# The second layer's conditioning product moved from VectorE, ScalarE and GpSimd to column groups of TensorE

## The chip, the core and the metric

The kernel runs on one core of one Trainium2 chip. The metric is the device time of one execution, in microseconds (us). Three executions of the kernel before took 2191.03, 2194.42 and 2195.73 us; the median is 2194.42 us.

A core has engines with a queue of instructions each: TensorE (PE in the profile, with PEld for its weight loads), VectorE (DVE), ScalarE (ACT), GpSimd (POOL) and SyncE (SP, which here only issues transfers). An engine takes its instructions in the order in which the program holds them; an instruction that waits for a semaphore holds everything behind it on its engine. GpSimd both computes and issues transfers, in one queue.

## The reference, cut to what matters

Two layers (`DEPTH = 2`) of a backbone over 512 latent and 256 context tokens, 1024 wide, in fp32. Each layer has six modulation vectors of 1024 values for each of two conditioning vectors:

```
mod_x = silu(c) @ ada_w[l] + ada_b[l]          # ada_w[l]: 1024 x 6144
mod_c = silu(c_ctx) @ ada_w[l] + ada_b[l]
sh1, sc1, g1, sh2, sc2, g2 = split_cols(mod, (D_MODEL,) * 6)
u   = modulate(rmsnorm(x, norm1_w[l]), sh1, sc1)
x   = x + g1 * mix(u)
x   = x + g2 * sq_relu_mlp(modulate(rmsnorm(x, norm2_w[l]), sh2, sc2), w_mlp1[l], w_mlp2[l])
```

The conditioning product is small in arithmetic (two rows times a 1024 x 6144 matrix) and reads 25 MB of `ada_w` for each layer.

## The kernel before, in words

Activations stand in SBUF as tiles of 128 rows. The big matrix products run on TensorE as three passes of a high and a low half (`mm3`, lines 302 to 305: high by high, low by high, high by low). Every weight slab is loaded by SP as a raw tile `wr`, copied to its high half `wh` by ScalarE (L139), and its low half `wl` is made by VectorE or GpSimd (L140). These pieces are handed out one by one (`W.tick()`) between the products.

The place that matters is the MLP of layer 0, which is a generator `mlp_gen`: for eight chunks of 512 hidden units a first product (`mlp1`, into PSUM tiles `ph`), and for six of them a second product in Strassen's form (`strassen`, seven products into PSUM tiles `st`, whose operands `ob` are made by VectorE and ScalarE from the hidden tile `hb`, L1192 to L1197, and whose results are added up by VectorE, L1226). GpSimd combines the Strassen weights (L152). After the sixth of these a `fold` adds the result to the residual, and the last two chunks follow.

While this MLP runs, the conditioning product of layer 1 is made beside it (lines 1331 to 1334). There are 12 pieces of 512 columns (`ada`, six vectors in two halves), each from two transfers of 1 MB (`ada_load`, L338, issued by GpSimd into a tile `adaw` of the pool `big`, which has 11 buffers that the MLP's tiles share). Each time that a piece yields, the `Filler` puts out a number of microseconds of MLP work:

```
for _ in chainup(*[ada(l + 1, v, c0, 512, ps, "t", wk, None, E1) for v in range(6) for c0 in (0, 512)]):
    fm.adv(8.0)
```

`E1` is ScalarE, so the pieces of layer 1 go through `ada_dve` (L310): the row of `silu(c)` is multiplied in by VectorE (L327, L329), eight instructions for each piece; the row of `silu(c_ctx)` by ScalarE (L323) and added up by GpSimd (L325). Both leave a 128 x 512 partial sum, `acc`, whose 128 rows TensorE then adds with a selector of ones (L356), in four column groups of 32 columns: `tile_position=(0, 32 * g)`. Then VectorE copies the result (`adar`, L371 or L376), and it is transposed (L380) into `cols` or written to DRAM (`grow`, L374).

In layer 0 most pieces take another way through the same function: L362 multiplies the loaded tile on TensorE, with `cT` (the two conditioning rows and 30 columns of zeros) as the stationary side, again in four column groups.

The order of the instructions on each engine is not written by hand. The framework's scheduler places them when the program is built, from the order in which the generators put them out and its own estimate of when each is ready.

Of the kernel before, what the change touches and what calls it, by code (L numbers as in the profile page):

```python
# [9 lines left out]
F32 = mybir.dt.float32  # L10
F32R = mybir.dt.float32r
I32 = mybir.dt.int32
AF = mybir.ActivationFunctionType
ALU = mybir.AluOpType
# [3 lines left out]
P = 128  # L18
DM = 1024
# [29 lines left out]
def kernel(  # L49
# [26 lines left out]
    nc = tc.nc  # L76
    V, A, T = nc.vector, nc.scalar, nc.tensor
# [5 lines left out]
    def bigt(name, dt=F32):  # L83
        return big.tile([P, 4, TOK], dt, name=name, tag="big")

    def flat(t):
        return t.rearrange("p a b -> p (a b)")

    class Weights:
# [73 lines left out]
        def next(self, key):  # L163
            i = self.i
            want, (src, *_) = self.plan[i][:2]
            assert want == key, (want, key)
            while self.bg and self.bg[0][0] <= i:
                self.tick()
            self.dma(i + 3)
            self.split(i + 2)  # L170
            self.i += 1
            k, n = src.shape[1], src.shape[2]
            return tuple(t[:, : k * n].rearrange("p (k n) -> p k n", k=k) for t in self.sp.pop(i))
# [131 lines left out]
        T.matmul(ps, al, bh, start=False, stop=last, **kw)  # L305

    lda = [None]
    E0, E1 = {(3, 0): V, (4, 0): V, (5, 0): V}, A

    def ada_dve(l, v, c0, wk, eng1):  # L310
        at = wk.tile([P, DM], F32, name=f"acc{l}{v}{c0}", tag="xn" if l else "jk", bufs=2 if l else 1)
        acc = [at[:, 0:512], at[:, 512:DM]]
        if eng1 is A:
            tm = wk.tile([P, DM], F32, name=f"acm{l}{v}{c0}", tag="xn", bufs=2)
        for s, (rv, ins) in enumerate(ada_load(l, v, c0, 512, nc.gpsimd)):
            lda[0] = getattr(ins, "ins", ins)
            for k in range(4):
                kk = 4 * s + k
                for st, eng in ((0, V), (1, eng1)):
                    w = cT[:, kk, st : st + 1]  # L320
                    if eng is A:
                        h = tm[:, 512 * (kk % 2) : 512 * (kk % 2) + 512] if kk else acc[st]
                        A.activation(out=h, in_=rv[:, k, :], func=AF.Copy, scale=w)  # L323
                        if kk:
                            nc.gpsimd.tensor_tensor(out=acc[st], in0=acc[st], in1=h, op=ALU.add)  # L325
                    elif kk == 0:
                        eng.tensor_scalar(out=acc[st], in0=rv[:, k, :], scalar1=w, scalar2=None, op0=ALU.mult)  # L327
                    else:
                        eng.scalar_tensor_tensor(out=acc[st], in0=rv[:, k, :], scalar=w, in1=acc[st], op0=ALU.mult, op1=ALU.add)  # L329
            yield None  # L330
        return acc

    def ada_load(l, v, c0, n, eng):
        kp = 2048 // n
        for s in range(KT // kp):
            rw = big.tile([P, 6, 512], F32, name=f"adaw{l}{v}{c0}{s}", tag="big")
            rv = rw.rearrange("p a b -> p (a b)")[:, : kp * n].rearrange("p (k n) -> p k n", k=kp)
            yield rv, eng.dma_start(out=rv, in_=wslab(ada_w[l], s * kp * P, kp, v * DM + c0, n))  # L338

    def ada(l, v, c0, n, ps_pool, ps_tag, wk, loads=None, eng1=None):  # L340
        G = n // P
        kp = 2048 // n
        gate = v in (2, 5)
        acc = None
        if eng1 is not None:
            g = ada_dve(l, v, c0, wk, eng1)
            while acc is None:
                try:
                    next(g)
                    yield 1.0  # L350
                except StopIteration as e:
                    acc = e.value
        pa = ps_pool.tile([P, 512], F32, name=f"ada{l}{v}{c0}", tag=ps_tag)
        for st in range(2 if acc else 0):
            for g in range(G):
                T.matmul(pa[32 * g : 32 * g + 32, :P], sel[:, 1 - st : 33 - st], acc[st][:, P * g : P * g + P],  # L356
                         start=(st == 0), stop=(st == 1 and not gate), skip_group_check=True, tile_position=(0, 32 * g))
        for s, (rv, ins) in enumerate(() if acc else loads or ada_load(l, v, c0, n, nc.gpsimd)):
            lda[0] = getattr(ins, "ins", ins)
            for k in range(kp):  # L360
                for g in range(G):
                    T.matmul(pa[32 * g : 32 * g + 32, :P], cT[:, kp * s + k, :], rv[:, k, P * g : P * g + P],  # L362
                             start=(s + k == 0), stop=(kp * s + k == KT - 1 and not gate), skip_group_check=True, tile_position=(0, 32 * g))
            yield 1.0
        row = wk.tile([P, P], F32, name=f"adar{l}{v}{c0}", tag="rt", bufs=2)
        if gate:
            for g in range(G):
                o = 16 + 8 * v + c0 // P + g
                T.matmul(pa[32 * g : 32 * g + 32, :P], wcol[l][:, o : o + 1].to_broadcast([P, 32]), ident, start=False, stop=True,
                         skip_group_check=True, tile_position=(0, 32 * g))  # L370
            V.tensor_copy(row, pa[:, :P])  # L371
            for g in range(G):
                o = c0 + P * g
                nc.gpsimd.dma_start(out=grow[l][v // 3, :, o : o + P], in_=row[32 * g : 32 * g + 2, :])  # L374
        else:
            V.tensor_copy(row[: 32 * G], pa[: 32 * G, :P])  # L376
            vi = {0: 0, 1: 1, 3: 2, 4: 3}[v]
            ks = slice(c0 // P, c0 // P + G)
            pt = ps_pool.tile([P, 512], F32, name=f"adat{l}{v}{c0}", tag=ps_tag)
            T.transpose(pt[:, : 32 * G], row[: 32 * G], ident[: 32 * G, : 32 * G])  # L380
            dst = cols[l][:, vi, ks, :]
            src = pt[:, : 32 * G].rearrange("p (g q) -> p g q", g=G)[:, :, 0:2]
            bias = wcol[l][:, 16 + 8 * v : 24 + 8 * v][:, ks]
            V.tensor_tensor(out=dst, in0=src, in1=bias.unsqueeze(2).to_broadcast([P, G, 2]), op=ALU.add)
            if v in (1, 4):
                nw = (wcol[l][:, 0:8] if v == 1 else wcol[l][:, 8:16])[:, ks]
                V.scalar_tensor_tensor(out=dst, in0=dst, scalar=1.0, in1=nw.unsqueeze(2).to_broadcast([P, G, 2]), op0=ALU.add, op1=ALU.mult)
        yield 0.5

    def load_rows(l, wk, eng):  # L390
        rows = wk.tile([68, P], F32, name=f"lrows{l}", tag="rt", bufs=2)
        for src, r in ((norm1_w, 0), (norm2_w, 8), (ada_b, 16), (pool_scale, 64)):
            n = src.shape[1] // P
            eng.dma_start(out=rows[r : r + n, :], in_=src[l].rearrange("(k p) -> k p", p=P))
        return rows

    def layer_consts(l, ps_pool, ps_tag, rows):
        pt = ps_pool.tile([P, 512], F32, name=f"lct{l}", tag=ps_tag)
        T.transpose(pt[:, :68], rows, ident[:68, :68])
        V.tensor_copy(wcol[l], pt[:, :68])  # L400
# [107 lines left out]
    def chainup(*gens):  # L508
        for g in gens:
            yield from g  # L510

    def layer(l, u_in):
# [7 lines left out]
        ps = Banks(es, f"psn{l}", g=6, r=2)  # L520
        wk = es.enter_context(tc.tile_pool(name=f"wk_n{l}", bufs=1, reuse_waits="tile"))
# [60 lines left out]
        rv = flat(bigt(f"rv{l}")).rearrange("p (t n) -> p t n", t=NT)  # L582
# [43 lines left out]
        if l == 0:  # L626
            for _ in chainup(*[ada(0, v, c0, 512, ps, "r", wk, None, E0.get((v, c0))) for v in (2, 3, 4, 5) for c0 in (0, 512)]):
                f1.adv(2.5)
# [6 lines left out]
        ps = Banks(es, f"psr{l}", g=3, r=5)  # L635
        esv = ExitStack()
        wkv = esv.enter_context(tc.tile_pool(name=f"wk_v{l}", bufs=1, reuse_waits="tile"))
        wk = es.enter_context(tc.tile_pool(name=f"wk_r{l}", bufs=1, reuse_waits="tile"))
# [303 lines left out]
        ps = Banks(es, f"psa{l}", g=3, s=1, m1=2, m2=1)  # L942
        wkt = es.enter_context(tc.tile_pool(name=f"wk_t{l}", bufs=2, reuse_waits="tile"))
        wk = es.enter_context(tc.tile_pool(name=f"wk_a{l}", bufs=2, reuse_waits="tile"))
# [182 lines left out]
        ps = Banks(es, f"pso{l}", g=6, t=2)  # L1127
        wk = es.enter_context(tc.tile_pool(name=f"wk_m{l}", bufs=2, reuse_waits="tile"))
# [39 lines left out]
        acc = {}  # L1168
# [139 lines left out]
        fm = Filler(mlp_gen())  # L1308
# [21 lines left out]
        g2 = load_g(1)  # L1330
        if not last:
            layer_consts(l + 1, ps, "t", load_rows(l + 1, wk, nc.gpsimd))
            for _ in chainup(*[ada(l + 1, v, c0, 512, ps, "t", wk, None, E1) for v in range(6) for c0 in (0, 512)]):
                fm.adv(8.0)
        un_ = None
        if not last:
            nh = [bigt(f"uh{l + 1}{q}", F32R) for q in range(2)]
# [57 lines left out]
    for l in range(DEPTH):  # L1395
        u = layer(l, u)
# [70 lines left out]
```

## Time and profile before

| | |
|---|---|
| median of three runs | 2194.42 us |
| the profiled execution | 2195.33 us, of which the span of the trace is 2193.4 us |
| TensorE busy | 2089.3 us, 95% of the span |
| VectorE, ScalarE, GpSimd busy | 1479.6, 919.4 and 759.0 us |
| TensorE's mean granted clock | 0.986 of full speed |
| layer 1's conditioning pieces | from about 770 to about 1160 us of the span |

Times in the trace count from the start of the span. A row of a group of instructions gives the source line, the engine, the operation, the tiles (out<-in), the shapes and the count, then the busy time and the mean duration of one in ns, then how long the engine sat idle just before them and what ended that wait. Durations of matmuls overlap their neighbours, so the cost of a row of matmuls is read from the distance between starts.

### The profile page before, as it was taken

The page shows a single profiled execution, that of the slowest core. Times are in us where ns is not written, and L with a number is a line of the kernel's source. Part 1 is how long each engine was busy: PE and PEld are TensorE (multiplying, and loading weights), DVE is VectorE, ACT ScalarE, POOL GpSimd, SP SyncE. Part 2 cuts the span into 40 slices and gives each one's busy share as a digit, 9 for nine tenths or more (in the row PEclk, how much of TensorE's full clock was granted, in tenths as well). Part 3 has the DMA queues.
Part 4 walks back from the last instruction along what each step waited for, and adds up shares of the span by engine and source line. Part 5 has one row for each costly group of instructions (what it writes and reads, how often), then busy time and mean ns, then how long its engine had stood idle before and what let it go on. Part 6 is the DMA issues. An engine that isn't in the chain of part 4 may idle for free.

```text
span 2193.4 us, 33041 instructions
## 1 busy us (share of the span) xinstructions
PE 2089.3 (95%) x12831; PEld 1795.4 (82%) x12831; DVE 1479.6 (67%) x2619; ACT 919.4 (42%) x1803; POOL 759.0 (35%) x565
## 2 busy tenths in 40 slices
PE   5999989999999999888899999998999999999999
PEld 5999968888888787777777888997888888888777
DVE  4697963454443777898989647469556467668883
ACT  3323323443432465544543325223354445545441
POOL 0252242212233455765572123433323453222300
PEclk8999999999999999999999999999999999999999
DMA  9741111111124533333334224211222254333241
GB/s 319 242 157 49 35 39 52 44 44 53 36 63 167 184 130 125 106 124 118 124 107 153 76 84 148 80 54 56 64 67 63 64 189 140 97 97 99 78 138 51
DMA packets 224597, 225.79 MB, mean 103 GB/s; under 512 B 8320, under 2 KB 180664, under 8 KB 224440
## 3 DMA queue, kind: packets, MB, share of 16 engines
q1 hardware_dynamic: 208744, 168.96, 25.0%
q0 software_dynamic: 15696, 54.71, 7.2%
q8 instruction: 101, 1.65, 0.3%
q14 instruction: 56, 0.46, 0.1%
HBM read 216.27 MB, written 7.37 MB: 102 GB/s over the span
## 4 chain that ended last, share of the span: by engine, by line
PE 38%; DVE 11%; issue 3%; ACT 1%; POOL 1%; DMA 1%; POOLq 0%; DVEq 0%; ACTq 0%
PE ph L305 4%; PE ph L304 4%; PE ph L303 3%; PE tg L303 3%; PE tg L304 3%; PE tg L305 3%; DVE wl L140 2%; PE pg L303 2%; PE pg L305 2%; PE pg L304 2%; PE st L303 1%; PE st L304 1%; DVE acc L1226 1%; PE st L305 1%; DVE acc L329 1%
## 5 line engine op out<-in xcount | busy, mean ns | idle before, releaser
L140 POOL TENSOR_TENSOR wl<-wr,wh 128x512 fp32r<-128x512 f32 x304 | 424.4, 1409 | 876.7 <-ACT wh L139 834.8
L139 ACT ACTIVATE wh<-wr 128x512 fp32r<-128x512 f32 x640 | 370.9, 624 | 494.0 <-issue 199.8
L140 DVE TENSOR_TENSOR wl<-wr,wh 128x512 fp32r<-128x512 f32 x336 | 265.7, 814 | 165.7 <-ACT wh L139 160.8
L304 PE MATMUL ph<-u2l,wh 128*128 128x512 f32 (+1 forms) x808 | 281.8, 349 | 1.9 <-DVE u2l L1380 1.9
L303 PE MATMUL ph<-u2h,wh 128*128 128x512 f32 (+1 forms) x808 | 281.6, 351 | 0.6 <-DVE acc L1226 0.3
L305 PE MATMUL ph<-u2h,wl 128*128 128x512 f32 (+1 forms) x808 | 280.4, 349 | 0.9 <-DVE wl L140 0.9
L303 PE MATMUL tg<-wh,uh 128*128 128x256 f32 x784 | 226.6, 289 | 3.0 <-DVE rt L1154 2.1
L304 PE MATMUL tg<-wl,uh 128*128 128x256 f32 x784 | 223.5, 285 | 0.0
L305 PE MATMUL tg<-wh,ul 128*128 128x256 f32 x784 | 222.7, 285 | 0.0
L303 PE MATMUL pg<-uh,wh 128*128 128x512 f32 (+1 forms) x576 | 208.8, 363 | 0.0
L305 PE MATMUL pg<-uh,wl 128*128 128x512 f32 (+1 forms) x576 | 207.5, 360 | 0.0
L304 PE MATMUL pg<-ul,wh 128*128 128x512 f32 (+1 forms) x576 | 207.4, 360 | 0.0
L152 POOL TENSOR_TENSOR wr<-wr,wr 128x1024 f32<-128x1024 f32 x48 | 123.1, 2565 | 218.0 <-DVE wl L140 200.3
L303 PE MATMUL st<-wh,ob 128*128 128x512 f32 x420 | 166.6, 401 | 16.2 <-DVE acc L1226 12.9
L304 PEld LDWEIGHTS ph<-u2l,wh 128*128 128x128 f32 x808 | 155.1, 192 | 21.9 <-DVE u2l L1380 2.5
L303 PEld LDWEIGHTS ph<-u2h,wh 128*128 128x128 f32 x808 | 154.6, 192 | 22.4 <-issue 2.7
L305 PEld LDWEIGHTS ph<-u2h,wl 128*128 128x128 f32 x808 | 155.2, 192 | 20.7 <-DVE wl L140 1.4
L304 PE MATMUL st<-wl,ob 128*128 128x512 f32 x420 | 165.4, 394 | 2.5 <-DVE wl L140 2.5
L305 PE MATMUL st<-wh,ob 128*128 128x512 f32 x420 | 165.2, 394 | 0.0
L325 POOL TENSOR_TENSOR acc<-acc,acm 128x512 f32<-128x512 f32 x84 | 129.7, 1544 | 80.5 <-ACT acm L323 70.7
L303 PEld LDWEIGHTS tg<-wh,uh 128*128 128x128 f32 x784 | 150.8, 192 | 5.4 <-DVE rt L1154 2.3
L329 DVE SCALAR_TENSOR_TENSOR acc<-adaw,cT,acc 128x512 f32<-128x512 f32 x126 | 148.9, 1200 | 5.3 <-DMA adaw<-in_ada_w_dram 4.1
(319 smaller groups left out, 4493.1 us busy)
## 6 DMA issues: line engine op xcount, KB each, us to landing
wr<-in_w_mlp_dram SPq DMA_DIRECT2D x136, 512.0 KB, 4.2
wr<-in_w_in_dram SPq DMA_DIRECT2D x88, 512.0 KB, 3.9
adaw<-in_ada_w_dram POOLq DMA_DIRECT2D x42, 1024.0 KB, 6.0
wr<-in_w_out_dram SPq DMA_DIRECT2D x32, 512.0 KB, 3.4
adaw<-in_ada_w_dram SPq DMA_DIRECT2D x6, 1024.0 KB, 15.6
wr<-in_w_ret_out_dram SPq DMA_DIRECT2D x16, 256.0 KB, 2.8
wr<-in_w_pool_out_dram SPq DMA_DIRECT2D x16, 256.0 KB, 2.9
wr<-in_w_attn_out_dram SPq DMA_DIRECT2D x32, 128.0 KB, 2.8
```

Source lines behind the costliest of these rows:

```text
L139: A.activation(out=box["h"][:, a:b], in_=r[:, a:b], func=AF.Copy)
L140: eng.tensor_tensor(out=box["l"][:, a:b], in0=r[:, a:b], in1=box["h"][:, a:b].bitcast(F32), op=ALU.subtract)
L152: nc.gpsimd.tensor_tensor(out=t, in0=self.raw[a], in1=self.raw[b], op=f)
L303: T.matmul(ps, ah, bh, start=first, stop=False, **kw)
L304: T.matmul(ps, ah, bl, start=False, stop=False, **kw)
L305: T.matmul(ps, al, bh, start=False, stop=last, **kw)
L325: nc.gpsimd.tensor_tensor(out=acc[st], in0=acc[st], in1=h, op=ALU.add)
L329: eng.scalar_tensor_tensor(out=acc[st], in0=rv[:, k, :], scalar=w, in1=acc[st], op0=ALU.mult, op1=ALU.add)
L1226: V.tensor_tensor(out=av, in0=bk, in1=av, op=ALU.add)
```

## The change

The pieces of layer 1 no longer go through `ada_dve`: they take the way of L362, with full fp32 operands, in four column groups. In that way, for layer 1 alone, the generator now yields after it has issued a transfer and before the products that read it, so that one step of MLP work stands between them; and the PSUM tile is taken only then. A step is now 10 us of MLP work and not 8. The scalar-engine branch of `ada_dve` is gone; layer 0's three VectorE pieces stay as they were.

```
-    E0, E1 = {(3, 0): V, (4, 0): V, (5, 0): V}, A
+    E0 = {(3, 0): V, (4, 0): V, (5, 0): V}
...
-                    if eng is A:
-                        h = tm[:, 512 * (kk % 2) : 512 * (kk % 2) + 512] if kk else acc[st]
-                        A.activation(out=h, in_=rv[:, k, :], func=AF.Copy, scale=w)
-                        if kk:
-                            nc.gpsimd.tensor_tensor(out=acc[st], in0=acc[st], in1=h, op=ALU.add)
-                    elif kk == 0:
+                    if kk == 0:
...
-        pa = ps_pool.tile([P, 512], F32, name=f"ada{l}{v}{c0}", tag=ps_tag)
+        pa = None
+        if acc or not l:
+            pa = ps_pool.tile([P, 512], F32, name=f"ada{l}{v}{c0}", tag=ps_tag)
...
         for s, (rv, ins) in enumerate(() if acc else loads or ada_load(l, v, c0, n, nc.gpsimd)):
             lda[0] = getattr(ins, "ins", ins)
+            if l:
+                yield 1.0
+                pa = pa or ps_pool.tile([P, 512], F32, name=f"ada{l}{v}{c0}", tag=ps_tag)
             for k in range(kp):
                 for g in range(G):
                     T.matmul(pa[32 * g : 32 * g + 32, :P], cT[:, kp * s + k, :], rv[:, k, P * g : P * g + P],
                              start=(s + k == 0), stop=(kp * s + k == KT - 1 and not gate), skip_group_check=True, tile_position=(0, 32 * g))
-            yield 1.0
+            if not l:
+                yield 1.0
...
-            for _ in chainup(*[ada(l + 1, v, c0, 512, ps, "t", wk, None, E1) for v in range(6) for c0 in (0, 512)]):
-                fm.adv(8.0)
+            for _ in chainup(*[ada(l + 1, v, c0, 512, ps, "t", wk) for v in range(6) for c0 in (0, 512)]):
+                fm.adv(10.0)
```

The built programs differ only between the first of these pieces and the end of layer 0's MLP: on TensorE the first 4068 and the last 4608 rows of the order are the same, apart from line numbers (L362 of before is L360 of the changed file, L338 is L331, L374 is L373).

On TensorE, at the eighth of the twelve pieces (`ada13512`: layer 1, vector 3, the half from column 512), the program before held the selector's four column groups for both rows, eight products, among those of a first MLP product (`ph`):

```order
L305 MATMUL ph0512_10063<-u2h00_7242,wl127_9948 128x256
L303 MATMUL ph0512_10063<-u2h01_7243,wh127_9947 128x256
L356 MATMUL ada13512_9969<-acc13512_9812,sel_66 32x128 x8
L304 MATMUL ph0512_10063<-u2l01_7245,wh127_9947 128x256
L305 MATMUL ph0512_10063<-u2h01_7243,wl127_9948 128x256
```

The changed program holds a run of 16 products for each of the piece's two transfers, among those of Strassen products (`st`):

```order
L305 MATMUL st0310_10226<-wh131_10102,ob030_10215 128x512
L360 MATMUL ada13512_10236<-adaw135120_10147,cT_68 32x128 x16
L303 MATMUL st0311_10255<-wh131_10102,ob030_10215 128x512
...
L305 MATMUL st0312_10267<-wh133_10263,ob031_10216 128x512
L360 MATMUL ada13512_10236<-adaw135121_10253,cT_68 32x128 x16
L303 MATMUL st0350_10280<-wh134_10288,ob031_10216 128x512
```

In place of one read of finished sums there are now two reads of tiles that a transfer fills; 48 rows of 128x512 products stand between the two.

On GpSimd, at about the same place, the program before held the additions `acc` among the splits `wl`, the Strassen combinations `wr` and the issues of the transfers:

```order
L325 TENSOR_TENSOR acc13512_9812<-acc13512_9812,acm13512_9813 128x512
L140 TENSOR_TENSOR wl128_9993<-wr131_9937,wh128_9992 128x512
L325 TENSOR_TENSOR acc13512_9812<-acc13512_9812,acm13512_9813 128x512
L152 TENSOR_TENSOR wr137_10258<-wr135_10166,wr134_10090 128x1024
L140 TENSOR_TENSOR wl129_10029<-wr132_9983,wh129_10028 128x512
L152 TENSOR_TENSOR wr138_10341<-wr136_10243,wr137_10258 128x1024
L338 DMA adaw1401_10123<-in_ada_w_dram 128x4x512
L338 DMA adaw145120_10278<-in_ada_w_dram 128x4x512
L325 TENSOR_TENSOR acc140_10046<-acc140_10046,acm140_10047 128x512
L140 TENSOR_TENSOR wl130_10106<-wr133_10013,wh130_10105 128x512
L325 TENSOR_TENSOR acc140_10046<-acc140_10046,acm140_10047 128x512 x6
```

The changed program holds the rest without the additions:

```order
L152 TENSOR_TENSOR wr137_10166<-wr135_10087,wr134_10004 128x1024
L140 TENSOR_TENSOR wl129_9939<-wr132_9893,wh129_9938 128x512
L152 TENSOR_TENSOR wr138_10234<-wr136_10151,wr137_10166 128x1024
L331 DMA adaw135120_10147<-in_ada_w_dram 128x4x512
L140 TENSOR_TENSOR wl130_10020<-wr133_9923,wh130_10019 128x512
L152 TENSOR_TENSOR wr140_10322<-wr136_10151,wr135_10087 128x1024
L152 TENSOR_TENSOR wr142_10405<-wr139_10313,wr138_10234 128x1024
L331 DMA adaw135121_10253<-in_ada_w_dram 128x4x512
L331 DMA adaw1400_10451<-in_ada_w_dram 128x4x512
L331 DMA adaw1401_10541<-in_ada_w_dram 128x4x512
L140 TENSOR_TENSOR wl138_10438<-wr141_10396,wh138_10437 128x512
```

The issues of the transfers stand later against the MLP's work than before (`adaw135120` is issued where the program before was at `adaw1401`). In the built program the issue of `adaw135121` waits until the 16 products on `adaw135120` have freed its buffer, and two combinations stand ahead of it.

## Rows read from the trace of the kernel before

**Rows 1.** The page: the span, and each engine's busy time.

```profile
span 2193.4 us, 33041 instructions
PE 2089.3 (95%) x12831; PEld 1795.4 (82%) x12831; DVE 1479.6 (67%) x2619; ACT 919.4 (42%) x1803; POOL 759.0 (35%) x565
```

**Rows 2.** Windows: stretch, length, busy time of PE, PEld, DVE, ACT, POOL (count), clock, DMA.

```profile
770.00:1160.00 390.00, 354.88 (x1976) 294.25 (x1975) 338.08 (x358) 206.55 (x365) 241.18 (x163) 0.97 0.36 118
...
1800.00:1900.00 100.00, 98.41 (x515) 84.02 (x514) 68.75 (x111) 58.90 (x112) 32.43 (x21) 1.00 0.39 119
1900.00:2000.00 100.00, 98.40 (x433) 80.81 (x432) 78.50 (x112) 49.63 (x89) 24.03 (x10) 1.00 0.36 110
```

**Rows 3.** Windows of 20 us within the first of these stretches.

```profile
880.00:900.00 20.00, 14.50 (x75) 12.15 (x74) 17.76 (x15) 9.58 (x18) 17.19 (x11) 0.91 0.38 131
...
1020.00:1040.00 20.00, 15.40 (x86) 12.86 (x86) 17.98 (x19) 8.81 (x15) 15.98 (x10) 0.89 0.39 142
```

**Rows 4.** Waits of PE from 760 to 1160: total us, times, longest.

```profile
PE ada L356 <- DVE acc L329: 10.4, 4, 4.6
PE st L303 <- DVE acc L1226: 8.6, 5, 3.1
PE ada L356 <- POOL acc L325: 6.6, 3, 2.3
PE adat L380 <- DVE adar L376: 5.6, 3, 3.6
```

**Rows 5.** Groups of instructions by line from 770 to 1160, conditioning lines alone.

```profile
L325 POOL TENSOR_TENSOR acc<-acc,acm 128x512 f32<-128x512 f32 x84 | 129.7, 1544 | 80.5 <-ACT acm L323 70.7 <-issue 6.5
L329 DVE SCALAR_TENSOR_TENSOR acc<-adaw,cT,acc 128x512 f32<-128x512 f32 x84 | 113.0, 1346 | 5.3 <-DMA adaw<-in_ada_w_dram 4.1
...
L323 ACT ACTIVATE acm<-adaw,cT 128x512 f32<-128x512 f32 x84 | 58.6, 717 | 56.3 <-DMA adaw<-in_ada_w_dram 27.0 <-POOL acc L325 20.4 <-PE ada L356 9.0
...
L356 PE MATMUL ada<-acc,sel 128*32 128x128 f32 x192 | 10.6, 310 | 17.0 <-DVE acc L329 10.4 <-POOL acc L325 6.6
```

**Rows 6.** Timeline of PE in layer 0's own pieces: start us, us, instruction, count.

```profile
66.64 1.94 PE L362 MATMUL ada<-adaw,cT 128*32 128x128 f32 x32
68.51 0.39 PE L303 MATMUL tg<-wh,uh 128*128 128x256 f32 x1
...
82.72 1.06 PE L362 MATMUL ada<-adaw,cT 128*32 128x128 f32 x32
83.70 0.38 PE L305 MATMUL tg<-wh,ul 128*128 128x256 f32 x1
...
85.96 0.28 PE L305 MATMUL tg<-wh,ul 128*128 128x256 f32 x1
86.17 1.08 PE L362 MATMUL ada<-adaw,cT 128*32 128x128 f32 x32
...
104.14 0.43 PE L356 MATMUL ada<-acc,sel 128*32 128x128 f32 x8
104.50 0.39 PE L305 MATMUL tg<-wh,ul 128*128 128x256 f32 x1
```

**Rows 7.** The tile adaw from 770 to 1160: its issues, waits for it, its landing.

```profile
L338 POOL DMA_DIRECT2D adaw<-in_ada_w_dram x22: 751/768/808, 809.2 to 1116.7; - x22
...
  DMA adaw<-in_ada_w_dram: 42.8, 15
...
DMA to landing us min/median/max: 5.5/5.7/9.2
```

**Rows 8.** Timeline of PE in the same stretch: the pace of the MLP's products.

```profile
1045.95 0.39 PE L305 MATMUL ph<-u2h,wl 128*128 128x512 f32 x1
1046.18 0.40 PE L303 MATMUL ph<-u2h,wh 128*128 128x512 f32 x1
...
1048.35 0.28 PE L304 MATMUL ph<-u2l,wh 128*128 128x256 f32 x1
1048.46 0.28 PE L305 MATMUL ph<-u2h,wl 128*128 128x256 f32 x1
```

More of the change, by code (lines that the diff above doesn't have):

```diff
@@ L307 @@
     lda = [None]
-    E0, E1 = {(3, 0): V, (4, 0): V, (5, 0): V}, A
+    E0 = {(3, 0): V, (4, 0): V, (5, 0): V}
     def ada_dve(l, v, c0, wk, eng1):
-        at = wk.tile([P, DM], F32, name=f"acc{l}{v}{c0}", tag="xn" if l else "jk", bufs=2 if l else 1)
+        at = wk.tile([P, DM], F32, name=f"acc{l}{v}{c0}", tag="jk", bufs=1)
         acc = [at[:, 0:512], at[:, 512:DM]]
-        if eng1 is A:
-            tm = wk.tile([P, DM], F32, name=f"acm{l}{v}{c0}", tag="xn", bufs=2)
         for s, (rv, ins) in enumerate(ada_load(l, v, c0, 512, nc.gpsimd)):
```

## The prediction

> **What bounds the kernel now.** I read the page's busy times first: TensorE is busy 95% of the span [rows 1], so only two things can shorten the kernel: less work on TensorE, or less of the remaining 5%, about 104 us, in which it is idle. The windows by stretch come next, because an average hides where those 104 us lie. In the stretch from 770 to 1160, where layer 1's conditioning runs beside layer 0's MLP, TensorE is busy 354.88 of 390.00 us: 35.1 us idle, a third of the whole, or 9.0% [rows 2]. Its granted clock there is 0.97 on average. The two windows of layer 1's own MLP, the same kind of work without conditioning beside it, show 3.2 us idle in 200 (1.6%) and a clock of 1.00 [rows 2]. These are my control for what the stretch would be without the load on the other engines. The windows of 20 us show how the clock is lost: where TensorE was busy 14.50 or 15.40 of 20 us, the clock granted is 0.91 and 0.89 [rows 3], a part of each window at the 1.2 GHz level.
>
> The waits name the causes. TensorE waited 10.4 us for VectorE's partial sums and 6.6 us for GpSimd's, both at the selector product L356; 5.6 us for the copy that follows (L376); and 8.6 us for VectorE to free a PSUM bank of the Strassen product [rows 4]. The groups by line show why VectorE and GpSimd are late: they spend 113.0 and 129.7 us of the 390 on these sums, and ScalarE 58.6 us [rows 5], which leaves VectorE busy 338.08 us of 390 [rows 2]. In the control it is busy 147.25 of 200.
>
> **The change part by part.** I sum against the profiled execution, 2195.33 us, 0.9 us above the median of 2194.42.
>
> *The idle time.* L356 goes, and with it its 17.0 us of waits [rows 5]. The wait at L380 should nearly go, since VectorE has no long queue of sums ahead of the copy and, in the new order, some twenty matmuls stand between the last product and the transpose. The waits for PSUM banks fall to what the control has. I take the whole at the control's rate: 1.6% of 390 is 6.2, so 35.1 - 6.2 = 28.9 us go. The bounds: at most all 35.1; at least the 17.0 at L356 alone, if the other waits stay.
>
> *The clock.* 0.97 over 390 us is 11.7 us of lost full speed; TensorE was busy 91% of it, so 10.6 us of work come back if the clock stays at 1.00 as in the control. Bounds 0 and 11.7. I take 10.6, because the low windows are those with the long idle times that the change removes.
>
> *The new work on TensorE.* Each of 12 pieces has 8 row blocks by 4 column groups, 32 products, and each product is two instructions: 768 instructions in 24 runs of 32. The same form, with the same four groups, stands in layer 0's timeline: 32 instructions from 82.72 to the next start at 83.70, which is 0.98 us [rows 6]. The step into such a run is dearer too: 85.96 to 86.17 is 0.21 us, where a 256-column product paces at 0.11 to 0.12 [rows 6, 8], so 0.09 us more. 24 x (0.98 + 0.09) = 25.7 us. That is the likely value since form and size agree; there is little spread in it as long as the clock is full, and at half clock it doubles.
>
> Whether four groups really run side by side is the question on which this price hangs. In the rows, 32 instructions in two groups take 1.87 us (66.64 to 68.51) and in four groups 0.98 us [rows 6]: the step from two to four halves the time. The Trainium skill, "TensorE: Matmul & The Clock Gate", Measured speedup vs the span model, lists smaller gains for packing: 2.38x with three column groups and 3.07x with four row groups. By 3.07 in place of 4, my estimate for a run rises by a factor of 4/3.07, which would be 0.29 us more for each of 24 runs, 7 us in all, and a total of 2184. The trace doesn't agree with so large a loss between two and four groups, so I keep the rows' price.
>
> *The removed work on TensorE.* L356: 192 instructions. A run of eight takes 0.36 us to the next start (104.14 to 104.50) [rows 6] and 0.09 to enter; the order before has 14 such runs, and five of 16, which are 0.22 us longer (eight instructions at 0.98/32 less the way out, some 0.028 each). 19 x 0.45 + 5 x 0.22 = 9.7 us. Net new work: 25.7 - 9.7 = 16.0 us.
>
> *The waits that it adds.* Now TensorE itself reads the transferred tile, and all of the MLP is queued behind a run that waits. Before, VectorE and ScalarE took that wait: 42.8 us at 15 places [rows 7]. A transfer needs 0.77 us to issue and 5.7 to land [rows 7], 6.5 in all. One step ahead means that some 48 MLP products stand between issue and use. Their pace is 0.23 us at 512 columns and 0.11 to 0.12 at 256 [rows 8]; 48 Strassen products take 11.0 us, and 24 of each kind 8.3 us, so the cover is 1.8 to 4.5 us longer than needed. It is thin in three or four of the 24, where the pool `big` gives up a buffer only when the run before is done, and there a combination or two on GpSimd (L152) can stand ahead of the issue. I take 4 us, bounds 0 and 42.8, near the lower end because the earlier request is what the old 42.8 us lacked. If GpSimd holds at an issue, the splits and combinations behind it are late; it has 129.7 us less to do, so that is covered. The last transfer waits for VectorE's fold, about two slabs of the next first product ahead of its use: covered by some 20 us.
>
> *The rest.* A step of 10 us spreads the 36 steps over more MLP work, and the last piece now ends behind the fold. Nothing reads it before layer 1's MLP or the next norm, so I put this at nothing; its cover is the two last chunks. VectorE, ScalarE and GpSimd lose 113.0 and more, 58.6 and 129.7 us, of which nothing counts beside the idle time already taken.
>
> Sum: 2195.3 - 28.9 - 10.6 + 16.0 + 4 = 2175.8. I say 2176 us.
>
> **The rivals.**
>
> *Late transfers become TensorE's waits (slower).* If the 24 issues stay as late against their use as before, the 42.8 us land on TensorE. For it: the pool has 11 buffers and the issue waits for a matmul or VectorE to free one; GpSimd's queue is in order. Against it: before, the sums were queued right behind the issue, now a step stands between. Price: 2176 - 4 + 42.8 = 2215. It decides from about 1 us for each of the 24 runs, which eats the 20 us gained.
>
> *Only the waits at L356 go.* The MLP's own waits and the clock stay, since the Strassen stage also loads VectorE by itself. 17.0 + 5.6 saved, 16.0 + 4 added: 2193, no change. For it: TensorE still waits for L1226 in the control. Against it: the control's total is small.
>
> *More comes back.* All idle time and all of the clock: 2195.3 - 35.1 - 11.7 + 16.0 = 2164.5. For it: VectorE falls well below the control's load. Against it: the control, at a lighter load on GpSimd, still has 1.6%.
>
> *The change doesn't do what it says.* If the four groups ran one behind another in this place, a run would take 4 x 0.98 us: 24 x 2.94 = 71 us more, 2247. The rows of the same form in layer 0 speak against it.
>
> **How the numbers follow.** Forecast 0.60 (its own range 2169 to 2184); more comes back 0.15; only L356's waits 0.15; late transfers 0.08; groups in sequence 0.02. What a measurement of this kernel can tell from no change is about 0.2%, or 4.4 us: faster is below 2190.0, slower above 2198.8. The case of L356 alone lies half in "faster" and half in "same"; add a little for things that I don't see. Faster 0.83, same 0.09, slower 0.08. The range runs from 2163, just under the case in which everything comes back, to 2193, the case in which only the waits at L356 go: the remainder outside is the slower cases and a tenth for surprises.
>
> **What would show it.** In the changed profile, TensorE idle from 770 to about 1180 should be 6 to 12 us, with the clock at 0.99 or 1.00; L360 in layer 1 should have 768 instructions at 27 to 31 ns from start to start, and waits for `adaw` of a few us in all. VectorE should be busy near 215 us of that stretch and GpSimd near 110, and the MLP of layer 1 should be as before. I am wrong if L360 waits more than 15 us for transfers, if a run takes over 1.3 us, or if the waits for VectorE at L1226 or for splits at L140 grow in the place of those at L356.

## The result and the profile after

The changed kernel takes 2159.37 us (median of 4 runs, 2159.27 to 2160.67); the kernel before, in the same session, 2193.9 us. The ratio is 0.9844, with a 95% interval from 0.983 to 0.9857: 34.5 us less, where 18.4 were forecast (2194.42 to 2176). The direction was right, the size was not: the time lies below the range.

The page of the changed kernel, with its span and busy times, which answers to [rows 1]:

```profile
span 2157.6 us, 33841 instructions
...
PE 2091.7 (97%) x13407; PEld 1803.8 (84%) x13407; DVE 1323.2 (61%) x2523; ACT 860.0 (40%) x1707; POOL 614.9 (29%) x481
```

TensorE's busy time is nearly what it was (2089.3 before), although it has taken over the product. What shrank is the time in which it was idle: 104.1 us before, 65.9 after. The windows, with the columns of [rows 2], say where:

```profile
770.00:1160.00 390.00, 390.00 (x2629) 328.70 (x2628) 218.74 (x313) 160.78 (x290) 105.39 (x74) 1.00 0.38 124
1800.00:1900.00 100.00, 98.43 (x512) 84.02 (x511) 66.55 (x104) 59.20 (x112) 23.05 (x13) 1.00 0.31 94
1900.00:2000.00 100.00, 97.67 (x428) 79.82 (x427) 82.23 (x119) 48.20 (x86) 22.73 (x10) 1.00 0.36 111
```

In the stretch from 770 to 1160 TensorE is busy for 390.00 of 390.00 us, at a granted clock of 1.00. Layer 1's MLP, the control of the prediction, still idles 1.6% and 2.3%. VectorE and GpSimd came out near the forecast (218.74 and 105.39 us against 215 and 110), VectorE by luck: the forecast took its other instructions to stay as they were, but the stretch now holds 104 of its splits (L140) at a mean of 690 ns, where it held 85 at 1029. The two windows that lost most before [rows 3] are full:

```profile
880.00:900.00 20.00, 20.00 (x113) 17.45 (x112) 5.46 (x9) 6.72 (x14) 4.79 (x2) 1.00 0.27 92
1020.00:1040.00 20.00, 20.00 (x119) 17.55 (x118) 8.26 (x10) 8.10 (x16) 4.79 (x2) 1.00 0.09 27
```

All the waits of TensorE from 760 to 1160, where the four largest kinds alone made 31.2 us [rows 4], are now two of the norm at the stage's entry:

```profile
PE xt L1367 <- ACT un L1371: 1.5, 1, 1.5
PE ph L304 <- DVE u2l L1379: 1.0, 1, 1.0
```

The waits for VectorE's PSUM release and for the copy `adar` went together with those at L356. A run of 16 products, 32 instructions, in the timeline of TensorE answers to [rows 6]:

```profile
864.75 0.39 PE L305 MATMUL st<-wh,ob 128*128 128x512 f32 x1
865.07 1.08 PE L360 MATMUL ada<-adaw,cT 128*32 128x128 f32 x32
866.08 0.50 PE L303 MATMUL st<-wh,ob 128*128 128x512 f32 x1
866.42 0.40 PE L304 MATMUL st<-wl,ob 128*128 128x512 f32 x1
```

The run takes 1.01 us to the next start; the step into it is 0.32 us where the Strassen products pace at 0.23, so 0.09 more, and the step out 0.34, so 0.11 more. The tile `adaw`, which answers to [rows 7], shows who waits now:

```profile
L331 POOL DMA_DIRECT2D adaw<-in_ada_w_dram x21: 748/766/818, 807.5 to 1147.3; - x21
its engine sat idle before it (us, times) until:
  PE ada L360: 58.2, 6
...
DMA to landing us min/median/max: 5.5/6.0/8.8
```

There is no row in which TensorE waits for `adaw`. GpSimd holds for 58.2 us at the issues, until products have freed a buffer, and nothing on TensorE is late for it.

To sum the stage I take the same two events in each trace: the start of the last eight `xt` transposes of the norm ahead of layer 0's MLP, and the first store `xs` behind it. Before:

```profile
777.40:1314.10 536.70, 500.21 (x2671) 415.64 (x2671) 438.14 (x485) 250.70 (x446) 275.48 (x185) 0.98 0.34 110
```

After:

```profile
777.10:1279.60 502.50, 502.50 (x3246) 423.92 (x3245) 282.98 (x389) 192.13 (x348) 133.95 (x101) 1.00 0.36 118
```

The stage is 34.2 us shorter. TensorE's idle time goes from 36.5 to 0.0 us. Its busy time grows by 2.3: the MLP's products, the same in number, are busy 12.0 us less (491.6 and 479.5 us over the groups `ph`, `st`, `tg`), which I put down to the higher clock: 0.98 over 536.7 us is some 11 us. What is left, 14.3 us, I take as the net new work. Outside the stage 1.6 us more went, which I don't explain.

### The profile page after: what moved, and what is told of

Read it like the earlier page. It is cut to its first block, busy times and chain, and to the rows that moved or that the text cites. A ratio compares the mean times of both kernels' runs of the same rounds, so it can differ in the third digit from the quotient of the medians.

```text
span 2157.6 us, 33841 instructions
## 1 busy us (share of the span) xinstructions
PE 2091.7 (97%) x13407; PEld 1803.8 (84%) x13407; DVE 1323.2 (61%) x2523; ACT 860.0 (40%) x1707; POOL 614.9 (29%) x481
## 4 chain that ended last, share of the span: by engine, by line
PE 81%; DVE 13%; issue 2%; ACT 2%; DMA 1%; POOL 0%; SPq 0%; DVEq 0%; ACTq 0%; POOLq 0%
PE ph L303 7%; PE ph L304 7%; PE ph L305 7%; PE tg L304 5%; PE tg L303 5%; PE tg L305 5%; PE pg L303 5%; PE pg L305 5%; PE pg L304 5%; PE st L303 4%; PE st L304 3%; PE st L305 3%; PE pb L304 3%; PE pb L303 3%; PE pb L305 3%; PE m L1099 2%
## 5 line engine op out<-in xcount | busy, mean ns | idle before, releaser
L140 POOL TENSOR_TENSOR wl<-wr,wh 128x512 fp32r<-128x512 f32 x304 | 415.2, 1379 | 938.8 <-ACT wh L139 904.3
L140 DVE TENSOR_TENSOR wl<-wr,wh 128x512 fp32r<-128x512 f32 x336 | 238.1, 731 | 254.9 <-ACT wh L139 254.8
L152 POOL TENSOR_TENSOR wr<-wr,wr 128x1024 f32<-128x1024 f32 x48 | 116.7, 2430 | 259.1 <-DVE wl L140 220.0
L304 PEld LDWEIGHTS tg<-wl,uh 128*128 128x128 f32 x784 | 150.9, 193 | 2.7 <-POOL wl L140 2.0
L305 PEld LDWEIGHTS tg<-wh,ul 128*128 128x128 f32 x784 | 150.3, 192 | 1.3 <-issue 1.2
```

What stands on the lines that cost most here:

```text
L140: eng.tensor_tensor(out=box["l"][:, a:b], in0=r[:, a:b], in1=box["h"][:, a:b].bitcast(F32), op=ALU.subtract)
L152: nc.gpsimd.tensor_tensor(out=t, in0=self.raw[a], in1=self.raw[b], op=f)
L304: T.matmul(ps, ah, bl, start=False, stop=False, **kw)
```

## The experiments

The theories. **A**: the sums' load on VectorE, ScalarE and GpSimd made these engines late for the MLP, and all of TensorE's idle time came from that. **A2**, a sharper form: GpSimd's additions lengthen VectorE's own instructions. **B**: the wider step, 10 us and not 8. **C**: the request one step early. **D**: not the load, but where the selector products stood, too close behind the last sum.

### The load put back, with nobody waiting for it

The changed kernel, and ahead of each run of its products the old sums of layer 1 into extra tiles `xa` and `xm` that nobody reads. In `load_all` all of them, in `load_dve` VectorE's row, in `load_actpool` ScalarE's and GpSimd's:

```
+            if l:
...
+                for k in range(4):
+                    kk = 4 * s + k
...
+                        V.scalar_tensor_tensor(out=xa[:, :512], in0=rv[:, k, :], scalar=cT[:, kk, 0:1], in1=xa[:, :512], op0=ALU.mult, op1=ALU.add)
...
+                    A.activation(out=hx, in_=rv[:, k, :], func=AF.Copy, scale=cT[:, kk, 1:2])
...
+                        nc.gpsimd.tensor_tensor(out=xa[:, 512:], in0=xa[:, 512:], in1=hx, op=ALU.add)
             for k in range(kp):
```

> The changed kernel with the old sums computed as well (eight instructions on VectorE, eight on ScalarE and seven on GpSimd for each of the 12 pieces, into tiles that nobody reads; so the load is back but no TensorE instruction waits for it by name). Theory A: the MLP's helpers are late again; TensorE idles 10 to 20 us in the stretch at lines of the MLP (L303 behind L1225, splits, transfers) and loses some clock: 12 to 30 us slower, 2171 to 2190. Rival D (only the selector products that read the sums made TensorE idle, by their place in its order): within 3 us of 2159.4.

> The changed kernel with VectorE's half of the old sums alone computed as well (eight instructions for each of 12 pieces, into tiles that nobody reads). With all three engines loaded it was 2201.3. Theory A1 (VectorE is the engine whose lateness reaches TensorE: it frees the PSUM banks, makes the Strassen operands and half of the splits): 15 to 30 us slower than 2159.4, with TensorE idle at L1225's bank release. Theory A2 (it is GpSimd beside VectorE that makes VectorE's own instructions longer, so one engine's load alone costs little): 0 to 8 us slower.

> The changed kernel with ScalarE's and GpSimd's half of the old sums alone computed as well, into tiles that nobody reads. Theory A1 (VectorE's own time is what counts): 0 to 8 us slower than 2159.4. Theory A2 (GpSimd's load is what counts, through longer VectorE instructions, late Strassen combinations and late issues of the transfers): 15 to 35 us slower, VectorE's splits (L140) at 950 to 1050 ns in place of 700.

Measured: `load_all` 2201.32 us (ratio to before 1.0032, 1.0019 to 1.0045), `load_dve` 2170.78 (0.99, 0.9885 to 0.9915), `load_actpool` 2171.21 (0.9899, 0.9882 to 0.9915). The window of `load_all`:

```profile
770.00:1160.00 390.00, 375.40 (x2452) 310.33 (x2450) 318.38 (x349) 198.10 (x353) 218.77 (x140) 0.99 0.33 110
```

The load alone, with no product behind it, brings back 14.6 us of idle time here and 41.9 us in all, more than the 12 to 30 of theory A. The stage between the same two events as above:

```profile
777.20:1320.70 543.50, 524.12 (x3246) 427.60 (x3245) 433.36 (x485) 249.74 (x444) 277.25 (x185) 0.99 0.34 109
```

It is 41.0 us longer than in the changed kernel, but only 19.4 of that are idle time, about half of the 36.5 of before. In the rest TensorE counts as busy, at a clock of 0.99 and with the products of layer 1 broken up: it enters them 49 times, in the changed kernel 26 times. So the load is shown as a cause, not as the cause of all the old idle time. The halves cost 11.4 and 11.8 us, each between what the two theories expected of it, and both together far more than their sum. That was not expected, and the next runs ask which pair does it.

### Which pair

The same, with GpSimd alone adding up the loaded rows (`load_pool`), ScalarE's copies alone (`load_act`), and VectorE's sums with GpSimd's additions but without ScalarE (`load_dvepool`):

```
...
+                    elif kk:
+                        nc.gpsimd.tensor_tensor(out=xa[:, 512:], in0=xa[:, 512:], in1=rv[:, k, :], op=ALU.add)
```

> The changed kernel, and beside its products GpSimd adds up the loaded rows of every piece as they are, 84 additions of 128x512, into a tile that nobody reads (no ScalarE copies, no sums on VectorE). Theory that GpSimd's additions slow VectorE's instructions: the whole cost of the ScalarE-and-GpSimd half (+11.8 us) is GpSimd's, so 2169 to 2173 us, with VectorE's splits at L140 at 850 to 1000 ns in place of 690. Rival, that the half cost time because ScalarE's 96 copies stand ahead of the MLP's own copies in ScalarE's queue: 2160 to 2164 us, splits near 700 ns.

> The changed kernel with the 96 scaled copies on ScalarE alone, into tiles that nobody reads. Theory that GpSimd's additions are what costs: ScalarE is at 160.78 of 390 us here, 59 us more leave it at 0.56, so 2159 to 2163 us and splits on VectorE near 700 ns. Rival, ScalarE's queue: 2168 to 2172 us.

> The changed kernel with the 96 sums on VectorE and 84 plain additions on GpSimd, nothing added to ScalarE. Theory that the two halves cost more together than apart because both lengthen VectorE's work (its own sums, and its instructions slowed by GpSimd): nearly all of the 41.9 us that both halves cost, 2192 to 2202 us, VectorE busy over 310 of 390 us. Rival, that ScalarE as third partner is needed for it: the sum of the parts alone, 2178 to 2184 us.

Measured: `load_pool` 2164.95 us (0.9866, 0.985 to 0.9883), `load_act` 2162.59 (0.9856, 0.9842 to 0.9871), `load_dvepool` 2210.88 (1.0074, 1.0058 to 1.0089). Over the changed kernel these are 5.6, 3.2 and 51.5 us. (The runs of these sections were taken beside executions of the kernel before with medians of 2193.08 to 2194.86 us, so a difference of 2 us between them says little.) ScalarE isn't needed: VectorE's sums alone cost 11.4 us and GpSimd's additions alone 5.6, together 51.5, so 34.5 us belong to the pair. I had expected 10 to 14 us for GpSimd alone, which was too much, and no more than 43 for the pair, which was too little. ScalarE adds something to GpSimd's part, 11.8 us for both against 5.6 and 3.2. (The profile of `load_pool` is of its longest run, 2169.9 us; the other three are within 2164.74 and 2165.05.) The stage of `load_dvepool` between the same two events:

```profile
776.00:1328.10 552.10, 520.72 (x3247) 428.43 (x3246) 436.46 (x485) 192.19 (x349) 291.17 (x185) 0.98 0.33 107
```

Its idle time is 31.4 us, near the 36.5 of before, and the clock is again the 0.98 of before. The longest waits of TensorE in it:

```profile
PE adat L392 <- DVE adar L388: 10.3, 3, 5.0
PE st L303 <- DVE acc L1238: 9.7, 11, 1.6
PE ada L373 <- DMA adaw<-in_ada_w_dram: 6.8, 1, 6.8
```

The first two are those of [rows 4] that the prediction had priced with the control. They wait for VectorE; with VectorE's sums alone the waits for it come to 0.5 us, with GpSimd's additions alone to 1.4. Of the 31.4 us, 22.5 end at VectorE by these rows and two small ones, 6.8 at the one late transfer and 1.7 at ScalarE. The added sums also read the transferred tiles, and so hold their buffers longer; no run separates that from the load itself. 31.4 us idle and the clock (0.02 of 552, some 11 us) make 42 of the 49.6 us that this stage is longer than the changed kernel's. The rest lies in part in the order: TensorE enters layer 1's products 42 times there, and 26 times in the changed kernel, and each further entry costs some 0.2 us by the steps read above, 3 us. The same holds for the 43 entries of `load_dve`, whose TensorE idles only 0.5 us in the stage; I can't split the remaining 8 us of that run.

What the pair does to each other stands in the trace of before already. GpSimd, and below it VectorE, at the place of the first window of [rows 3]:

```profile
889.46 9.07 POOL L325 TENSOR_TENSOR acc<-acc,acm 128x512 f32<-128x512 f32 x5
```

```profile
890.24 1.78 DVE L140 TENSOR_TENSOR wl<-wr,wh 128x512 fp32r<-128x512 f32 x1
891.95 2.04 DVE L1192 TENSOR_TENSOR stt<-stt,hb 128x768 f32<-128x768 f32 x1
893.91 5.96 DVE L329 SCALAR_TENSOR_TENSOR acc<-adaw,cT,acc 128x512 f32<-128x512 f32 x4
899.78 0.69 DVE L140 TENSOR_TENSOR wl<-wr,wh 128x512 fp32r<-128x512 f32 x1
```

While five additions run on GpSimd, to 898.53, VectorE's split takes 1.78 us, about as long as one of them (9.07 / 5 = 1.81); the first split behind them takes 0.69. The tiles' rows (min/median/max in ns) say which instructions are hit. The sums of before, whose mean is in [rows 5]:

```profile
L329 DVE SCALAR_TENSOR_TENSOR acc<-adaw,cT,acc x84: 737/1381/2882, 779.4 to 1133.5; 128x512 f32<-128x512 f32 x84
```

The splits of before, by line in the same stretch:

```profile
L140 DVE TENSOR_TENSOR wl<-wr,wh 128x512 fp32r<-128x512 f32 x85 | 85.4, 1029 | 19.2 <-ACT wh L139 14.2 <-POOL acc L325 4.9
```

In the changed kernel the split:

```profile
L140 DVE TENSOR_TENSOR wl<-wr,wh x104: 671/684/868, 785.5 to 1159.5; 128x512 fp32r<-128x512 f32 x104
```

With GpSimd's additions alone (`load_pool`), the split, and the Strassen addition, one of whose two inputs is in PSUM:

```profile
L140 DVE TENSOR_TENSOR wl<-wr,wh x99: 675/693/3083, 790.4 to 1159.5; 128x512 fp32r<-128x512 f32 x99
```

```profile
L1234 DVE TENSOR_TENSOR acc<-st,acc x97: 671/681/692, 859.0 to 1158.9; 128x512 f32<-128x512 f32 x97
```

Most splits take what they took, and some up to 3083 ns: the mean goes from 690 to 1005, not the median. The addition that reads PSUM never moves. VectorE's sums, first alone (`load_dve`), then with GpSimd's additions beside them (`load_dvepool`):

```profile
L366 DVE SCALAR_TENSOR_TENSOR xa<-adaw,cT,xa x74: 734/747/2771, 780.1 to 1158.5; 128x512 f32<-128x512 f32 x74
```

```profile
L366 DVE SCALAR_TENSOR_TENSOR xa<-adaw,cT,xa x70: 735/1631/2937, 779.0 to 1151.8; 128x512 f32<-128x512 f32 x70
```

The median goes from 747 to 1631 ns, and GpSimd's additions in that run have a median of 1624: the two engines take turns, one instruction each. The trace of before can be sorted the same way: of its 84 sums in the stretch, the 29 that run beside no instruction of GpSimd take 754 ns at most, and the other 55 have a median of 1672. So the 1346 ns of the sums in [rows 5] were no property of the instruction, but of its neighbour. Against 747 ns for a sum and 684 for a split, some 80 of VectorE's 338.08 us were waiting that looks like work: 50 in the 84 sums, 29 in the 85 splits at 1029. The Trainium skill, "SBUF — State Buffer", Who interferes with whom, has the rule: a VectorE instruction with two inputs in SBUF contends with a GpSimd instruction that reads SBUF, the first to start keeps the other out until it ends, and one with a single SBUF input, outside VectorE's two-port modes, is not touched. The trace agrees in all three points: the pace of 1631 beside 1624 ns, the splits' maximum of 3083, and 671 to 692 for the addition from PSUM.

### The other theories

`step8`, the changed kernel with the old step (theory B), and `no_early`, with the products put out in the step of their request (theory C):

```
-                fm.adv(10.0)
+                fm.adv(8.0)
```

```
             if l:
-                yield 1.0
                 pa = pa or ps_pool.tile([P, 512], F32, name=f"ada{l}{v}{c0}", tag=ps_tag)
...
-            if not l:
-                yield 1.0
+            yield 1.0
```

> The changed kernel with steps of 8 us of MLP work in place of 10, all else as changed. Theory A (the sums' load on VectorE, ScalarE and GpSimd made the MLP's own helpers late, and without it TensorE has no reason to idle in this stretch): within 2 us of the changed kernel's 2159.4, idle on TensorE in the stretch under 2 us. Rival B (the wider spacing of the transfers is what took the idle time away): 5 to 10 us slower, with waits for adaw on TensorE.

> The changed kernel with the yield behind the products again, so that a transfer is requested in the step that reads it. Rival C (the early request is what kept transfers off TensorE's path): TensorE waits for adaw in most of the 24 runs, 20 to 43 us in all, 2180 to 2205. Theory A says that the request is not where the 34 us came from; the scheduler can still place the products later in TensorE's order, so 0 to 5 us slower, 2159 to 2165, with under 5 us of waits for adaw.

Measured: `step8` 2160.54 us (0.9847, 0.983 to 0.9863), the same as the changed kernel; B falls. `no_early` 2165.96 (0.9875, 0.986 to 0.989), 6.6 us more. TensorE's only wait in the stage of `no_early`:

```profile
PE ada L359 <- DMA adaw<-in_ada_w_dram: 3.2, 1, 3.2
```

So the early request is worth some 6 us, of which one wait for a transfer is half. The scheduler places the products late by itself, and the 42.8 us of [rows 7] don't appear on TensorE either way.

`sums_late`, the kernel before with one more step between the last sum and the selector products (theory D; the step is 6 us, so that the pieces spread over the same work):

```
+        if l:
+            yield 1.0
         pa = ps_pool.tile([P, 512], F32, name=f"ada{l}{v}{c0}", tag=ps_tag)
         for st in range(2 if acc else 0):
...
-                fm.adv(8.0)
+                fm.adv(6.0)
```

> The kernel before with one more step between the last sum and the selector products that read it (steps of 6 us in place of 8, so that the 48 steps cover the same MLP work). Rival D (the place of the selector products in TensorE's order cost the 17.0 us and part of the clock): 15 to 25 us faster than before, 2169 to 2179. Theory A (the load makes the helpers late, and TensorE stands wherever it next needs one): 0 to 8 us faster, 2186 to 2194, the waits at L356 gone or halved and those at the MLP's own lines grown.

Measured: 2199.88 us (1.003, 1.0019 to 1.0041), slightly slower than before, where D expected 15 to 25 us less and A 0 to 8 less. Its four largest waits of TensorE, from 760 to 1160, beside [rows 4]:

```profile
PE adat L382 <- DVE adar L378: 10.0, 3, 6.2
PE ada L358 <- DVE acc L329: 6.7, 2, 5.5
PE st L303 <- DVE acc L1228: 6.2, 8, 2.2
PE ada L358 <- POOL acc L325: 4.5, 1, 4.5
```

The waits at the selector fall from 17.0 to 11.2 us, others take their place (the copy `adar` from 5.6 to 10.0), and TensorE's busy time in the stretch is 354.49 us as against 354.88. The wait for the loaded engine was moved here and came back elsewhere: D falls. (The shorter step changes the order as well, and A's small gain did not come either.)

`twice`: the changed kernel, each run followed by as many products of the same form (32 instructions) against a stationary tile of zeros.

```
+            for k in range(kp if l else 0):
+                for g in range(G):
+                    T.matmul(pa[32 * g : 32 * g + 32, :P], cz, rv[:, k, P * g : P * g + P],
...
```

> The changed kernel with every run of 32 instructions followed by 32 more of the same form against a stationary tile of zeros (the result stays the same). Price of the products as the rows had it: 24 x 32 x 27.7 ns = 21.3 us more, 2180.7. If the rivals' price of packing in place of the rows held (four groups at 3.07x), 28 us more, 2187. If TensorE has spare time left in the stretch that I do not see, less than 15 us more.

Measured: 2181.13 us (0.9943, 0.9928 to 0.9957), 21.8 more, near the 21.3 expected from layer 0's rows. The stage is 20.3 us longer, and TensorE is busy through all of it:

```profile
776.90:1299.70 522.80, 522.80 (x4014) 444.88 (x4013) 282.88 (x389) 193.36 (x348) 134.59 (x101) 1.00 0.35 114
```

20.3 us over 768 instructions are 26.4 ns each, no more than in the rows of layer 0, where four groups took half the time of two: the four groups do run side by side here, and TensorE's work now counts in full.

### Two attempts at a faster version

`e0_none` also moves layer 0's three VectorE pieces to TensorE (`E0 = {}`). `one_run` requests both transfers of a piece, a step apart, and then puts out its 32 products together.

```
-    E0 = {(3, 0): V, (4, 0): V, (5, 0): V}
+    E0 = {}
```

```
+        if l:
+            loads = []
+            for r in ada_load(l, v, c0, n, nc.gpsimd):
+                loads.append(r)
+                yield 1.0
         for s, (rv, ins) in enumerate(() if acc else loads or ada_load(l, v, c0, n, nc.gpsimd)):
...
             if l:
-                yield 1.0
                 pa = pa or ps_pool.tile([P, 512], F32, name=f"ada{l}{v}{c0}", tag=ps_tag)
```

> The changed kernel with layer 0's three VectorE pieces also multiplied on TensorE. Their stretch (60 to 140 us) has DMA busy at 0.74 and TensorE idle 2 of 80 us, so there is little for theory A to win: 3 more pieces at 1.8 to 2.1 us on TensorE less their selector products are 4 us more, and up to 3 us of waits less: 2158 to 2164. If the load on VectorE costs there what it did in layer 1's pieces (34 us for 12), 5 to 9 us faster, 2150 to 2154.

> The changed kernel with both transfers of a piece requested ahead, a step each, and then all 64 products of a piece put out together, so that TensorE enters 12 times rather than 24 where the scheduler keeps them whole. Price of an entry by the rows of before 0.09 us and the way out as much: up to 2 us saved, 2156 to 2159 us, if all runs stay whole. Rival: the transfers are requested no earlier and the buffers are held longer, so that products wait for them: 2160 to 2168 us.

Measured: 2165.91 us (0.9876, 0.9861 to 0.9891) and 2165.12 (0.9867, 0.9852 to 0.9882), both some 6 us slower than the changed kernel. From 60 to 140 us, where layer 0's pieces run, TensorE idles 0.96 us with the three pieces on VectorE and 0.88 without, so there was nothing to win; the move costs 6.5 us, 2.5 more than the products were priced at. In `one_run` TensorE enters layer 1's products 28 times by the trace, not 12, so no entries were saved; it waits for one transfer, 1.1 us, and the rest of what it loses is open. Neither beats the change.

## Why the prediction was wrong

- **Idle time: the step that failed.** The prediction said "I take the whole at the control's rate: 1.6% of 390 is 6.2, so 35.1 - 6.2 = 28.9 us go". All 35.1 went, and 1.4 more behind the stretch. The control was no measure of the stage. The prediction also took the 113.0 and 129.7 us that VectorE and GpSimd spent on the sums as work, and did not ask why an instruction took 1346 ns; that the two engines hold each other up has no place in it. Part of the control's 3.2 us was not the MLP's: 1.6 lie in the waits at `st`, the other 1.6 at `xt` and `u2l`, the norm at its entry. And VectorE is busy there for 0.74 of the time, in the changed stage for 0.56. That this share explains the rest was argued, not tested; what the runs do show is that the pair of VectorE's sums and GpSimd's additions makes 31.4 us of idle time, and each of the two alone at most 3.4. The change took both away at once. Its own splits and combinations on GpSimd still hold VectorE up now and then (an operand `ob` takes 3059 ns where the median is 954), at no cost to TensorE.
- **The waits added: 4 us forecast, 0 measured.** The reasoning from 48 products of cover held; the three or four thin places that the prediction allowed for did not show. GpSimd took the waiting, 58.2 us, at its issues.
- **The clock: 10.6 forecast, 12.0 measured** over the whole stage. The step was right: the granted clock is 1.00 in the stage, where the long idle times are gone.
- **Net work: 16.0 forecast, 14.3 measured.** The column groups were read rightly from layer 0's rows; `twice` gives 26.4 ns per instruction. The price of a run was too low: 1.01 us, 0.09 for the step in and 0.11 for the step out make 1.21, where 1.07 was forecast, because the step out was put at nothing. It was left out for the removed runs at L356 too (105.17 to 105.39 us in the trace of before, 0.10 over the pace), so that part of the two errors cancels, by luck. The 7 us more that the prediction worked out from a smaller gain of packing did not come (its total there should read 2183, not 2184).
- **The sum.** From the profiled spans, 2193.4 and 2157.6: 36.5 + 12.0 - 14.3 + 1.6 = 35.8 us. The forecast was 28.9 + 10.6 - 16.0 - 4 = 19.5. Of the 16.3 between, 7.6 are the idle time, 4.0 the waits, 1.7 the work, 1.6 what lies outside the stage and 1.4 the clock. All the errors have one sign.
- **The rivals.** "More comes back", 2164.5, was the right case and held 0.15. It had against it that "the control, at a lighter load on GpSimd, still has 1.6%". Its own time was 5 us too high, and the range ended just under it: with the idle time and the clock at their bounds it left no room for errors of the terms around them, here 1.7 us of work, 1.6 outside the stage, 1.4 of idle time behind the stretch and 0.3 of clock. Late transfers, only L356's waits, and groups in sequence are refuted by the rows above, and none of the signs that the prediction named for being wrong appeared.

## What to carry to other kernels

Before VectorE's busy time is taken as its work, compare the mean of an instruction with its minimum: 1346 beside 737 ns was a sign here that another engine was in its way, and taking that engine's work off returned more than the removed instructions. A stage's idle time is not to be priced from another stage that has other loads; here the change removed both partners of a contention, and the whole of the idle time went. A wait that stands at one line can be a symptom: moved, it came back at the next reader of the same engine.

## What was not expected of the hardware

VectorE and GpSimd take turns, instruction by instruction, where VectorE reads two tiles in SBUF: a median of 747 ns became 1631. The cost to TensorE is not additive: 11.4 us for one partner, 5.6 for the other, 51.5 for both. Why `load_dvepool` costs more than `load_all`, which has ScalarE's copies on top, is open; GpSimd's additions there don't wait for a copy. Full fp32 products in four column groups of TensorE cost 26.4 ns per instruction in a stage without idle time.
